# Two layers with sixteen experts each: second layer's results through DRAM, turns grouped anew, residual scale moved

## The chip, the core and the metric

The kernel runs on one core of a Trainium2 chip. Its engines are TensorE (PE; its weight loads are listed apart as PEld), VectorE (DVE), ScalarE (ACT), GpSimd (POOL) and SyncE (SP), which here issues most of the DMAs. Each engine works through its own instructions in order; a DMA queue (SPq, ACTq, POOLq) is fed by the engine that issues the DMAs, in the order of that engine's program. The metric is the device time of one execution in microseconds (us).

## The reference, cut to what matters

Two layers work on 512 latent tokens and 256 context tokens, with 1024 channels. A layer is a mixer (a projection, a recurrent scan, a long convolution and gates), a residual step with a layer norm, then a mixture of experts and a second residual step with a layer norm:

```python
def moe_ffn(h, w_router, router_bias, w_gate, w_up, w_down):
    scores = jax.nn.softmax(h @ w_router, axis=-1)           # 16 experts, 4 groups of 4
    ...                                                       # best group, then its top 2 experts; wts sum to 1
    def expert_block(args):
        xblk, e = args
        return (jax.nn.silu(xblk @ w_gate[e]) * (xblk @ w_up[e])) @ w_down[e]
    ...
    return (y_slots.reshape(n_tok, TOP_K, d) * wts[..., None]).sum(1)

def post_norm(x, s, g, b):                                    # ALPHA = 4 ** 0.25
    return layer_norm(ALPHA * x + s, g, b)                    # layer_norm scales by g and adds b

xl = post_norm(xl, mod_l[2] * mix_l, ln_g[l, 0], ln_b[l, 0])  # after the mixer
...
xl = post_norm(xl, mod_l[5] * yf, ln_g[l, 1], ln_b[l, 1])     # after the experts
```

`mod_l[5]` is the gate of the expert sub-layer, a row of 1024 numbers; the context has a row of its own. Layer 1 computes experts for the 512 latent tokens only, layer 0 for all 768. Every expert has three 1024 x 1024 float32 matrices.

## The kernel before, in words

Each layer runs through projection, scan, merge and experts. In the projection, 1 MB or 0.5 MB pieces of weights come in; ACT casts each to the high part (`hi`, L588), DVE subtracts for the low part (`lo`, L589), and PE multiplies in three passes (L593 to L595 or L848 to L855). ACT takes the sigmoid of the mixer's gates (L1056) and copies rows of modulation (`mrow`, L710) that PE then uses (L722).

**Experts.** The 16 experts are ranked by load. A table `CAPS` gives each rank a number of rows: layer 0 has 96, 256, 192, three of 160, four of 96 and six of 64; layer 1 has 96, 192, 128, five of 96 and eight of 64. A table `TURN` says which ranks are worked side by side. `(2,), (11, 10)` means rank 2 beside a pair: two 64-row experts that share a unit of 128 rows. A unit is up to 128 rows of tokens of one expert or pair. Layer 0 has eight turns, and so has layer 1. A turn gathers the rows of its tokens (POOL, L1874), transposes them, and goes through six chunks per expert: two of the gate matrix, two up (L1950), two down (L1953). In layer 0, 128-row units are worked in three passes from high and low parts. Each chunk needs two buffers of weights, `raw`, of 1 MB each, that SP loads (`weights`); they come from a ring of `RAW` buffers, 5 in layer 0 and 10 in layer 1, and a buffer is loaded again when PE is through with it. A layer loads 192 of them, 201.3 MB.

**Results.** A unit's result rows go back to their tokens in one of two ways. Units of the last `LATE` turns are multiplied by their gates and spread by a one-hot matrix `sel`: for each block of 128 tokens and each half of the channels PE multiplies the high and the low part (L2034, L2035) into `pt`, and DVE adds that to `xs` (L2037), which holds the residual stream. `LATE` is 1 in layer 0 and 99 (all turns) in layer 1. Units of other turns are written to DRAM (`yd`, by the ACT queue, L2074), without the gate. In the last turn of layer 0, `early` has POOL gather two such rows per token (L1772), add them (L1780), multiply by the gate row of the token's kind (L1781) and add to `xs` (L1782). After the second token block the row `grow[1]` is turned into a difference (L1784), from which DVE builds the gates of the last unit's rows (L2050).

**After the experts.** `finish` normalises. In layer 0 POOL then multiplies by the norm's scale and adds its offset (L1818, L1819) for each of four latent blocks, and SP stores that to DRAM (`xd`, L1820), from where layer 1's merge reads it as residual. Layer 1's projection has begun by then on PE, DVE and ACT.

## Time and profile before

| | |
|---|---|
| median of 3 runs | 3294.33 us (3290.19 to 3295.82) |
| profiled execution | 3294.88 us, span 3293.0 us |
| PE busy | 2976.3 us (90%) |
| DVE busy | 1711.4 us (52%) |
| ACT busy | 1143.1 us (35%) |
| POOL busy | 556.0 us (17%) |
| DMA moved | 675.42 MB, mean 205 GB/s |
| expert weights (`raw<-in_w_exp`) | 384 DMAs of 1024 KB |

A busy share over the whole span says little here: the stages have different limits. The page's slices show PE at 90% or more and DMA between 300 and 395 GB/s in the two expert stages (about 1110 to 1765 us and 2670 to 3260 us), and DMA around 50 to 160 GB/s in most of the others. So the tables by stage and by turn below are the ones to read, with the waits and the timeline where a turn is longer than its PE work. A row's `<-` after an idle time names what ended it.

### The profile page before, as it was taken

What the parts mean: (1) busy time and instruction counts of PE and PEld (TensorE: products, weight loads), DVE (VectorE), ACT (ScalarE), POOL (GpSimd) and SP (SyncE); (2) the same over time, 40 slices, a digit from 0 to 9 for tenths busy, and PEclk for the clock granted to TensorE, in tenths of its full rate; (3) what the DMA queues carried; (4) which work ended last, traced back from release to release, by engine and by line L of the source; (5) the groups of instructions that cost most, each with busy time, mean ns of one, the idle gap of its engine ahead of it and who ended that gap; (6) DMA issues with size and microseconds to landing.
All of it is one profiled execution on the core that took longest, in us unless ns stands there. A gap on an engine that the chain in (4) does not pass through costs nothing. (4 is left out here: it accounts for less than half of the span.)

```text
span 3293.0 us, 61763 instructions
## 1 busy us (share of the span) xinstructions
PE 2976.3 (90%) x25406; PEld 2036.7 (62%) x25406; DVE 1711.4 (52%) x3074; ACT 1143.1 (35%) x2309; POOL 556.0 (17%) x436
## 2 busy tenths in 40 slices
PE   8999998988888899999965999989887979999996
PEld 5878865767676555666632767657665745445543
DVE  4466525787758433344407546467885652123343
ACT  3453215655422233344412433265543221111121
POOL 1001213334005100000036001153320210000000
PEclk9999998898999799999996999988898879999998
DMA  5453273111353789988894374431113489888795
GB/s 223 131 157 97 82 260 114 49 47 46 113 195 129 279 331 346 350 328 326 322 392 157 111 218 126 156 119 53 56 50 126 152 327 395 325 303 314 300 360 240
DMA packets 215206, 675.42 MB, mean 205 GB/s; under 512 B 70949, under 2 KB 98886, under 8 KB 163464
## 3 DMA queue, kind: packets, MB, share of 16 engines
q1 hardware_dynamic: 186120, 588.36, 49.4%
q10 hardware_dynamic: 22512, 61.55, 5.3%
q0 software_dynamic: 6288, 21.50, 1.9%
q8 instruction: 203, 3.33, 0.4%
q14 instruction: 83, 0.68, 0.1%
HBM read 615.03 MB, written 56.30 MB: 204 GB/s over the span
## 5 line engine op out<-in xcount | busy, mean ns | idle before, releaser
L1950 PE MATMUL acc<-raw,x 128*32 128x128 f32 (+1 forms) x7168 | 569.5, 333 | 13.5 <-DMA raw<-in_w_exp 12.4
L1950 PEld LDWEIGHTS acc<-raw,x 128*32 128x32 f32 (+1 forms) x7168 | 362.3, 125 | 207.5 <-issue 86.4
L589 DVE TENSOR_TENSOR lo<-raw,hi 128x1024 fp32r<-128x1024 f32 x190 | 230.0, 1230 | 294.9 <-ACT hi L588 282.6
L1953 PE MATMUL acc<-raw,a 128*64 128x512 f32 (+2 forms) x1376 | 300.3, 604 | 2.0 <-DMA raw<-in_w_exp 1.9
L588 ACT CAST hi<-raw 128x1024 fp32r<-128x1024 f32 x190 | 194.7, 1047 | 242.5 <-PE px L852 114.7
L1981 DVE TENSOR_TENSOR act<-acc,act 128x256 f32<-128x256 f32 (+2 forms) x98 | 42.0, 429 | 379.9 <-PE acc L1950 345.1
L848 PE MATMUL pl<-xh,hi 128*128 128x512 f32 x560 | 226.7, 405 | 0.1
L853 PE MATMUL pl<-xh,lo 128*128 128x512 f32 x560 | 223.9, 400 | 0.5 <-DVE lo L589 0.5
L849 PE MATMUL pl<-xl,hi 128*128 128x512 f32 x560 | 222.9, 398 | 0.0
L1953 PEld LDWEIGHTS acc<-raw,a 128*64 128x64 f32 (+2 forms) x1376 | 81.1, 130 | 168.0 <-issue 155.9
L1116 PE MATMUL gp<-gx,raw 128*128 128x512 f32 (+1 forms) x352 | 179.1, 628 | 1.2 <-ACT gs L1118 1.1
L1874 POOL DMA_INDIRECT xg<-hd,idx x31 | 32.0, 1031 | 756.1 <-PE pt L1892 678.5
L848 PEld LDWEIGHTS pl<-xh,hi 128*128 128x128 f32 x560 | 106.1, 189 | 37.6 <-issue 14.3
L1976 ACT ACTIVATE act<-acc 128x256 f32<-128x256 f32 (+2 forms) x98 | 38.0, 388 | 259.5 <-PE acc L1950 216.0
L853 PEld LDWEIGHTS pl<-xh,lo 128*128 128x128 f32 x560 | 106.5, 190 | 17.9 <-issue 9.2
L1999 ACT COPY a<-pt 128x256 f32<-128x256 f32 (+2 forms) x86 | 27.7, 350 | 255.4 <-PE pt L1994 248.5
L849 PEld LDWEIGHTS pl<-xl,hi 128*128 128x128 f32 x560 | 106.0, 189 | 15.8 <-issue 8.1
L311 PE MATMUL pO<-T,K 128*128 128x192 f32 (+1 forms) x320 | 83.4, 372 | 29.9 <-DVE T L330 29.3
L851 PE MATMUL px<-xh,hi 128*128 128x256 f32 x376 | 110.0, 293 | 0.0
L855 PE MATMUL px<-xh,lo 128*128 128x256 f32 x376 | 108.7, 290 | 0.0
L852 PE MATMUL px<-xl,hi 128*128 128x256 f32 x376 | 108.2, 288 | 0.4 <-DVE xl L589 0.3
L2037 DVE TENSOR_TENSOR xs<-pt,xs 128x512 f32<-128x512 f32 x116 | 75.8, 686 | 54.6 <-PE pt L2035 53.8
(611 smaller groups left out, 6200.2 us busy)
## 6 DMA issues: line engine op xcount, KB each, us to landing
raw<-in_w_exp SPq DMA_DIRECT2D x384, 1024.0 KB
mraw<-in_w_mod SPq DMA_DIRECT2D x64, 512.0 KB
raw<-in_w_in SPq DMA_DIRECT2D x36, 512.0 KB
rkk<-rkk SPq DMA_DIRECT2D x24, 768.0 KB
raw<-in_w_in ACTq DMA_DIRECT2D x34, 512.0 KB
mraw<-in_w_mod SPq DMA_DIRECT2D x12, 1024.0 KB
raw<-in_w_in SPq DMA_DIRECT2D x32, 256.0 KB
wb<-in_w_branch SPq DMA_DIRECT2D x32, 256.0 KB
```

What stands on the lines that cost most here:

```text
L311: nc.tensor.matmul(pO[:, jj, 0:192], lO, T[c][kO, j, 1, :], start=True, stop=True)
L588: self.nc.scalar.copy(hi, src)
L589: (engine or self.nc.vector).tensor_tensor(lo, src, f32(hi), ALU.subtract)
L848: mm(pl, hi[:, k], xh[:, k, L], start=f, stop=False)
L849: mm(pl, hi[:, k], xl[:, k, L], start=False, stop=False)
L851: mm(px, hi[:, k], xh[:, k, X], start=f, stop=False)
L852: mm(px, hi[:, k], xl[:, k, X], start=False, stop=False)
L853: mm(pl, lo[:, k], xh[:, k, L], start=False, stop=e)
L855: mm(px, lo[:, k], xh[:, k, X], start=False, stop=e)
L1116: nc.tensor.matmul(p[:, :n], raw[k // 4][:, k % 4], self.gx[:, k, a - T0:a - T0 + n], start=k == 0, stop=k == 7)
L1950: mm(a[w * g:w * g + w, 0:4 * w], x, raw[:, 4 * w * g:4 * w * g + 4 * w], start=k == 0, stop=k == 7)
L1953: mm(a[w * g:w * g + w], x, raw, start=k < G, stop=k >= 8 - G)
```

## The change

- **Turns.** Layer 0 has seven turns: the ranks of 256, 192 and 160 rows each run beside a pair, two with 160 beside 96, and the last is two experts of 96. Layer 1 has seven too: 192, 128 and 96 rows each beside a pair, two of 96 with 96, and a last turn of one pair. The ring of layer 0 has 6 buffers rather than 5.
- **Results of layer 1.** `LATE` is 1 in both layers. `yd` is a list with an array per layer. Layer 1 writes all results but the last unit's to DRAM, and gathers them in its last turn. In layer 0 the last turn has two units where it had one.
- **Gates.** Every unit's result is multiplied by its gate row before it is written or spread, so `early` has two operations per block rather than three, and the difference of the gate rows is formed ahead of the experts. `early` fetches 5 (layer 0) or 4 (layer 1) token blocks ahead rather than 3.
- **Residual scale.** Layer 0's `finish` stores the normalised rows as they are. A new block in layer 1's projection loads each of the four blocks of `xd` by the ACT queue into one buffer `t`, has POOL multiply and add, and stores it back by the ACT queue.
- The rows of `yd` that no unit writes are filled with zero for both layers (POOL's queue).

```diff
-RAW = 5, 10
+RAW = 6, 10
 AHEAD = 2, 2
 CAPS = ([96] + [256] + [192] + [160] * 3 + [96] * 4 + [64] * 6, [96] + [192] + [128] + [96] * 5 + [64] * 8)
-TURN = ([((0,),), ((2,), (11, 10)), ((1,), (13, 12)), ((3,), (6,)), ((4,), (7,)), ((5,), (8,)), ((9,),), ((15, 14),)],
-        [((0,),), ((15, 14),), ((1,), (13, 12)), ((2,), (3,)), ((4,), (5,)), ((6,), (7,)), ((11, 10),), ((9, 8),)])
-LATE = 1, 99
+TURN = ([((0,),), ((1,), (15, 14)), ((2,), (13, 12)), ((3,), (11, 10)), ((4,), (6,)), ((5,), (7,)), ((8,), (9,))],
+        [((0,),), ((1,), (15, 14)), ((2,), (13, 12)), ((3,), (11, 10)), ((4,), (5,)), ((6,), (7,)), ((9, 8),)])
+LATE = 1, 1
...
-SOME, YB, YW = 4, 1, (3, 2)
+SOME, YB, YW = 4, 1, (3, 3)
...
+        self.yd = [self.dt_([128 * rows_of(l)[2] + 1, 1024], f"yd{l}") for l in range(2)]
...
         mod_pools(GMR[l], 2)
+        if l == 1:
+            rs = s_mod.enter_context(tc.tile_pool(name="res", bufs=1))
+            lng, lnb = (rs.tile([128, 1024], F32, name=q, tag=q) for q in ("lng", "lnb"))
+            nc.scalar.dma_start(lng, A["ln_g"][0, 1][None, :].to_broadcast([128, 1024]))
+            nc.scalar.dma_start(lnb, A["ln_b"][0, 1][None, :].to_broadcast([128, 1024]))
+            for tb in range(2, 6):
+                t = rs.tile([128, 1024], F32, name="t", tag="t")
+                nc.scalar.dma_start(t, self.xd[tb])
+                nc.gpsimd.tensor_tensor(t, t, lng, ALU.mult)
+                nc.gpsimd.tensor_tensor(t, t, lnb, ALU.add)
+                nc.scalar.dma_start(self.xd[tb], t)
...
             def fetch(tb):
-                if tb % 3:
-                    y = f32(P["x"].tile([128, 8, 2, 128], F32R, name="x", tag="x256")).rearrange("p a b c -> p (a b c)")
+                if l == 0 and tb % 5:
+                    q = "x" if tb < 3 else "a"
+                    y = f32(P["x"].tile([128, 8, 2, 128], F32R, name=q, tag=q + "256")).rearrange("p a b c -> p (a b c)")
                     y = [y[:, 0:1024], y[:, 1024:2048]]
+                elif l == 1 and tb > 3:
+                    q = "x" if tb == 4 else "a"
+                    y = [P["x"].tile([128, 8, 128], F32, name=q, tag=q + "128", bufs=XB[l]).rearrange("p a b -> p (a b)") for i in range(2)]
                 else:
                     y = [P["x"].tile([128, 1024], F32, name="xg", tag="xg", bufs=XG[l]) for i in range(2)]
                 for i in range(2):
-                    nc.gpsimd.indirect_dma_start(out=y[i], out_offset=None, in_=self.yd, in_offset=bass.IndirectOffsetOnAxis(ap=slot[:, i, tb:tb + 1], axis=0))
+                    nc.gpsimd.indirect_dma_start(out=y[i], out_offset=None, in_=self.yd[l], in_offset=bass.IndirectOffsetOnAxis(ap=slot[:, i, tb:tb + 1], axis=0))
                 ys[tb] = y
 
-            for tb in range(3):
+            n = 5 - l
+            for tb in range(b0, b0 + n):
                 fetch(tb)
             for tb in blocks:
                 y = ys[tb]
                 op = nc.vector.tensor_tensor if tb in EARLY_V else nc.gpsimd.tensor_tensor
                 op(y[0], y[0], y[1], ALU.add)
-                op(y[0], y[0], grow[1 if tb < 2 else 0], ALU.mult)
                 op(self.xs[:, tb], y[0], self.xs[:, tb], ALU.add)
-                if tb == 1:
-                    nc.gpsimd.tensor_tensor(grow[1], grow[1], grow[0], ALU.subtract)
-                if tb + 3 < 6:
-                    fetch(tb + 3)
+                if tb + n < 6:
+                    fetch(tb + n)
...
                     self.normalise(sg, x, x, hs[tb])
                     if tb > 1:
-                        b = sg.tile([128, 1024], F32, name="b", tag="b")
-                        nc.gpsimd.tensor_tensor(b, x, lng, ALU.mult)
-                        nc.gpsimd.tensor_tensor(b, b, lnb, ALU.add)
-                        nc.sync.dma_start(self.xd[tb], b)
+                        nc.sync.dma_start(self.xd[tb], x)
...
         groups = TURN[l]
+        if on:
+            nc.gpsimd.tensor_tensor(grow[1], grow[1], grow[0], ALU.subtract)
...
-        def total(a, w, o, scale):
+        def total(a, w, o):
 
             t = P["a"].tile([128, 512], F32, name="sum", tag="y", bufs=3)[o:o + 64]
-            if w == 64:
-                nc.scalar.activation(t, a[64 - o:128 - o], AF.Copy, scale=scale)
-                return a[o:o + 64], t
             nc.scalar.copy(t, a[64 - o:128 - o])
             tt(t, a[o:o + 64], t, ALU.add)
+            if w == 64:
+                return t
             v = P["a"].tile([128, 512], F32, name="sum", tag="y", bufs=3)[o:o + 32]
-            nc.scalar.activation(v, t[32:64], AF.Copy, scale=scale)
-            return t[0:32], v
+            nc.scalar.copy(v, t[32:64])
+            tt(v, t[0:32], v, ALU.add)
+            return v
...
-                    sel[u] = P["x"].tile([128, 512], F32R, name="sel", tag="sel", bufs=3)
+                    sel[u] = P["x"].tile([128, 512], F32R, name="sel", tag="sel", bufs=1)
...
-                        if dst is None and l == 0:
+                        if l == 0:
                             g[u] = P["a"].tile([128, 512], F32, name="g", tag="act", bufs=ACT_BUFS[l])
                             stt(g[u][0:rows], self.grow[1][0:rows, H], own[:, 2:3], self.grow[0][0:rows, H], ALU.mult, ALU.add)
-                        elif dst is None:
+                        else:
                             g[u] = self.grow[0][:, H]
                 for (u, w, o, *_), a in zip(mine[j], acc):
                     rows, _, own, dst, _ = units[u]
                     R = slice(o, o + w)
                     y, by = out[u][R], own[R, 1:2]
                     if w < 128:
-                        a, t = total(a, w, o, 1.0 if dst is None else by)
-                    if dst is None:
-                        if w < 128:
-                            tt(t, a, t, ALU.add)
-                            a = t
-                        stt(y, a, by, g[u][R], ALU.mult, ALU.mult)
-                    elif w < 128:
-                        stt(y, a, by, t, ALU.mult, ALU.add)
-                    else:
-                        nc.scalar.activation(y, a, AF.Copy, scale=by)
+                        a = total(a, w, o)
+                    stt(y, a, by, g[u][R], ALU.mult, ALU.mult)
```

The line numbers of the changed kernel are shifted (L1950 became L1967, L1953 L1970, L1772 L1791, L1056 L1069).

On POOL, in the last turn of layer 0, this stands before; `xg` and `x` are gathered rows, `g_10143` and `g_10145` the gate rows of the latents and of the context:

```order
L1772 DMA xg<-yd,slot 128x1024 x2
L1772 DMA x<-yd,slot 128x1024 x4
L1780 TENSOR_TENSOR xg<-xg 128x1024
L1772 DMA xg<-yd,slot 128x1024
L1781 TENSOR_TENSOR xg<-xg,g_10145 128x1024
L1772 DMA xg<-yd,slot 128x1024
L1782 TENSOR_TENSOR xs<-xg,xs 128x1024
L1780 TENSOR_TENSOR x<-x 128x1024 x2
L1781 TENSOR_TENSOR x<-x,g_10145 128x1024
L1781 TENSOR_TENSOR x<-x,g_10143 128x1024
L1782 TENSOR_TENSOR xs<-x,xs 128x1024
L1784 TENSOR_TENSOR g_10145<-g_10145,g_10143 128x1024
```

And this now, in the same place:

```order
L1791 DMA xg<-yd_97,slot 128x1024 x2
L1791 DMA x<-yd_97,slot 128x1024 x4
L1791 DMA a<-yd_97,slot 128x1024 x4
L1800 TENSOR_TENSOR xg<-xg 128x1024
L1791 DMA xg<-yd_97,slot 128x1024
L1801 TENSOR_TENSOR xs<-xg,xs 128x1024
L1791 DMA xg<-yd_97,slot 128x1024
L1800 TENSOR_TENSOR x<-x 128x1024 x2
L1801 TENSOR_TENSOR xs<-x,xs 128x1024 x2
```

Ten gathers rather than six are issued ahead, the multiplications by gate rows are gone, and the subtraction no longer stands among them (it is now right behind the stage's first gather of token rows).

On ACT, at the end of layer 1's projection, this stands before; `pl` is PE's product for the latents, `hz` a row of modulation:

```order
L1056 ACTIVATE t_18423<-pl 128x512
L710 COPY mrow<-hz 128x512
L1056 ACTIVATE t_18483<-pl 128x512
L1056 ACTIVATE t_18517<-pl 128x512
L710 COPY mrow<-hz 128x512
L588 CAST hi<-raw 128x1024
L1056 ACTIVATE t_18576<-pl 128x512
```

And this now:

```order
L1052 DMA t<-xd 128x1024
L711 COPY mrow<-hz 128x512
L1055 DMA xd<-t 128x1024
L1069 ACTIVATE t_18666<-pl 128x512
L1052 DMA t<-xd 128x1024
L1069 ACTIVATE t_18700<-pl 128x512
L1055 DMA xd<-t 128x1024
L711 COPY mrow<-hz 128x512
L588 CAST hi<-raw 128x1024
L1052 DMA t<-xd 128x1024
L1055 DMA xd<-t 128x1024
L1069 ACTIVATE t_18759<-pl 128x512
```

The loads and stores of `t` stand among the sigmoids and the copies of `mrow`, the last of them ahead of the last sigmoid.

On PE, where a turn of layer 1 ends and the next begins, this stands before:

```order
L1953 MATMUL acc<-raw,a 64x512 x7
L2034 MATMUL pt<-yh,sel 128x512
L2035 MATMUL pt<-yl,sel 128x512
L2034 MATMUL pt<-yh,sel 128x512
L2035 MATMUL pt<-yl,sel 128x512
L1950 MATMUL acc<-raw,x 128x512
L2034 MATMUL pt<-yh,sel 128x512
L2035 MATMUL pt<-yl,sel 128x512
L2034 MATMUL pt<-yh,sel 128x512
L2035 MATMUL pt<-yl,sel 128x512
L1950 MATMUL acc<-raw,x 128x512 x7
```

And this now, at a turn's end in the same layer:

```order
L1970 MATMUL acc<-raw,a 64x512 x8
L1970 MATMUL acc<-raw,a 128x512 x8
L1970 MATMUL acc<-raw,a 64x512 x16
L1967 MATMUL acc<-raw,x 64x256 x8
L1967 MATMUL acc<-raw,x 32x128 x16
L1967 MATMUL acc<-raw,x 64x256 x8
L1967 MATMUL acc<-raw,x 32x128 x16
```

The products with `sel` that stood between the experts' products are gone.

## Rows read from the trace of the kernel before

**Rows 1.** page, the span

```profile
span 3293.0 us, 61763 instructions
```

**Rows 2.** windows of layer 1's experts: us, busy of each engine, PEclk, DMA share, GB/s

```profile
2669.70:3259.80 590.10, 580.37 (x4720) 301.19 (x4720) 184.88 (x334) 92.38 (x197) 11.77 (x12) 1.00 0.87 334
2711.70:2768.10 56.40, 54.20 (x373) 28.64 (x372) 17.55 (x31) 9.61 (x20) 2.75 (x3) 1.00 1.01 382
...
3069.00:3151.20 82.20, 82.20 (x951) 44.45 (x950) 31.63 (x57) 15.41 (x34) 0.00 (x0) 1.00 0.82 308
...
3204.60:3259.80 55.20, 49.90 (x346) 25.51 (x342) 16.19 (x26) 6.63 (x14) 0.00 (x0) 1.00 0.88 366
3180.00:3200.00 20.00, 18.75 (x109) 7.83 (x105) 5.70 (x9) 3.62 (x7) 0.00 (x0) 1.00 1.01 420
```

**Rows 3.** windows of layer 0's experts: the stage, then five turns

```profile
1110.60:1764.60 654.00, 611.00 (x5373) 384.35 (x5372) 241.34 (x286) 217.96 (x329) 74.75 (x48) 0.98 0.87 332
1154.40:1274.20 119.80, 112.51 (x673) 66.25 (x669) 39.78 (x45) 37.93 (x55) 3.73 (x3) 0.99 0.87 333
1274.20:1389.80 115.60, 115.07 (x657) 80.15 (x657) 39.55 (x42) 38.77 (x54) 2.78 (x3) 1.00 0.91 350
1389.80:1474.60 84.80, 84.79 (x923) 55.92 (x921) 41.81 (x47) 38.91 (x57) 2.72 (x3) 1.00 0.88 329
...
1640.60:1676.80 36.20, 35.96 (x466) 20.26 (x462) 5.79 (x10) 7.42 (x16) 0.00 (x0) 1.00 0.96 374
1676.80:1764.60 87.80, 54.77 (x344) 26.66 (x340) 22.51 (x26) 6.72 (x14) 56.86 (x31) 0.88 0.82 325
```

**Rows 4.** lines, layer 1's experts: the one-hot products

```profile
L2034 PE MATMUL pt<-yh,sel 96*128 96x512 f32 (+2 forms) x104 | 47.6, 468 | 8.4 <-ACT yh L588 7.8 <-DVE xs L2037 0.7
```

**Rows 5.** PE's timeline, two token blocks: start, us, instructions

```profile
2712.71 0.50 PE L2034 MATMUL pt<-yh,sel 96*128 96x512 f32 x1
...
2713.83 2.38 PE L1950 MATMUL acc<-raw,x 128*64 128x256 f32 x20
```

**Rows 6.** timeline of layer 0's last turn, POOL and DVE

```profile
1689.17 0.94 POOL L1772 DMA_INDIRECT xg<-yd,slot  x1 [0.30 <-issue]
...
1700.87 2.37 POOL L1780 TENSOR_TENSOR xg<-xg 128x1024 f32<-128x1024 f32 x1 [5.79 <-DMA xg<-yd,slot]
...
1728.77 1.41 DVE L2050 SCALAR_TENSOR_TENSOR g<-g,own,g 128x512 f32<-128x512 f32 x2 [31.70 <-POOL g L1784]
```

**Rows 7.** waits of PE, 1680 to 1780: total us, times, longest

```profile
PE pt L1994 <- DVE act L1981: 15.0, 4, 12.3
PE acc L1950 <- DMA raw<-in_w_exp: 12.0, 8, 1.9
```

**Rows 8.** timeline where layer 0 ends, POOL and DVE

```profile
1785.18 2.36 POOL L1818 TENSOR_TENSOR b<-xs,lng 128x1024 f32<-128x1024 f32 x1 [25.43 <-ACT xs L1380]
...
1787.93 2.38 DVE L1428 TENSOR_SCALAR q<-q 64x512 f32<-64x512 f32 x1
...
1803.65 4.67 DVE L589 TENSOR_TENSOR xl<-xt,xh 128x512 fp32r<-128x512 f32 x2
...
1815.40 0.41 DVE L1428 TENSOR_SCALAR q<-q 64x512 f32<-64x512 f32 x1
1815.73 0.68 DVE L589 TENSOR_TENSOR xl<-xt,xh 128x512 fp32r<-128x512 f32 x1
```

**Rows 9.** timeline of layer 1's gates, PE, ACT and POOL

```profile
2137.88 1.02 PE L722 MATMUL pq<-mrow,con 128*2 128x512 f32 x2 [0.70 <-ACT mrow L710]
...
2147.29 0.60 ACT L1056 ACTIVATE t<-pl 128x512 f32<-128x512 f32 x1 [8.52 <-issue]
...
2147.27 0.30 POOL L224 MEMSET PB<- 64x256 f32 x1 [39.24 <-PE pl L853]
```

**Rows 10.** timeline of SP's queue at the end

```profile
3282.53 0.33 SPq L1830 DMA_DIRECT2D out<-b  x1
```

**Rows 11.** window behind that store

```profile
3285.00:3286.00 1.00, 0.00 (x0) 0.00 (x0) 0.00 (x0) 0.00 (x0) 0.00 (x0) 0.50 0.02 8
```

More of the change, by code (lines that the diff above doesn't have):

```diff
@@ L659, in setup @@
         self.xd = self.dt_([6, 128, 1024], "xd")
-        self.yd = self.dt_([128 * rows_of(0)[2] + 1, 1024], "yd")
+        self.yd = [self.dt_([128 * rows_of(l)[2] + 1, 1024], f"yd{l}") for l in range(2)]
     def layer(self, l):
@@ L688, in zero_unused @@
         nc.gpsimd.memset(zero, 0.0)
-        base, nsb, first = rows_of(0)
-        used = {(b + 32 * i) // 32 for b, c in zip(base, CAPS[0]) for i in range(c // 32)}
-        for q in range(4 * first):
-            if q not in used and (q % 4 == 0 or q - 1 in used):
-                n = next((i for i in range(1, 4 - q % 4) if q + i in used), 4 - q % 4)
-                for h in range(2):
-                    nc.gpsimd.dma_start(self.yd[32 * q:32 * q + 32 * n, 512 * h:512 * h + 512], zero[0:32 * n])
-        for h in range(2):
-            nc.gpsimd.dma_start(self.yd[128 * first:128 * first + 1, 512 * h:512 * h + 512], zero[0:1])
+        for l in range(2):
+            base, nsb, first = rows_of(l)
+            used = {(b + 32 * i) // 32 for b, c in zip(base, CAPS[l]) for i in range(c // 32)}
+            for q in range(4 * first):
+                if q not in used and (q % 4 == 0 or q - 1 in used):
+                    n = next((i for i in range(1, 4 - q % 4) if q + i in used), 4 - q % 4)
+                    for h in range(2):
+                        nc.gpsimd.dma_start(self.yd[l][32 * q:32 * q + 32 * n, 512 * h:512 * h + 512], zero[0:32 * n])
+            for h in range(2):
+                nc.gpsimd.dma_start(self.yd[l][128 * first:128 * first + 1, 512 * h:512 * h + 512], zero[0:1])
     def mod(self, l, n, wr, sm, acc_, small, kk, dma, tag="mraw"):
@@ L1599, in unit @@
             return (rows, *((idx[0:rows, q:q + 1], own[0:rows, :, q]) if q else (idx0[0:rows], own0[0:rows])),
-                    None if q >= first else self.yd[128 * q:128 * q + rows], shared)
+                    None if q >= first else self.yd[l][128 * q:128 * q + rows], shared)
         units = {ranks: [unit(min(128, (len(ranks) * caps[ranks[0]]) - 128 * i), base[ranks[0]] // 128 + i, len(ranks) > 1) for i in range(-(-caps[ranks[0]] // 128))]
```

7 lines of the change are left out of this document (4 added, 3 removed).

## The prediction, made before the changed kernel ran

> **What bounds the kernel now.** I read the page first, then tables by stage, then the waits and timelines of the places that the change touches. The profiled execution took 3294.9 us, of which its span is 3293.0 [rows 1] and 1.9 lies around it; the median of the runs is 3294.3. The sum is made against 3294.9, and 0.6 goes off at the end. A run of this kernel can tell about 0.2%, 6.6 us, from no change.
>
> The two expert stages are 654.0 and 590.1 us. In layer 1 PE is busy 580.4 of 590.1 us at full clock, and DMA at a share of 0.87 and 334 GB/s [rows 2]: PE is the bound, but the weight stream is close behind, and in the turns of light experts both are full (382 GB/s at a share of 1.01). In layer 0 PE is busy 611.0 of 654.0 [rows 3]. Most of what is missing lies in the last turn, 87.8 us long with PE busy 54.8.
>
> **Layer 1: block adds go.** Today each 128-row result is spread over the tokens by one-hot products: 104 at L2034 [rows 4] and as many at L2035. Two blocks take 2712.71 to 2713.83, 1.12 us [rows 5], so a block costs PE 0.56 us, one after the other with the expert products. The change keeps the last unit's 8, so 96 x 0.56 = 53.8 us leave PE. The casts, DVE additions and one-hot rows that go with them lie beside PE and count nothing. In their place come 12 half-row writes of results and, in the last turn, 8 gathers (4.2 MB), with 8 POOL operations of 2.4 us [rows 6]: 19 us beside a turn of some 50, hidden.
>
> Then what is late next? PE would need 590 - 54 = 536 us. The stage moves 334 GB/s x 590.1 us = 197.1 MB; with 5.5 MB of writes and 4.2 MB of gathers it is 206.8 MB. At the 420 GB/s of one stretch that is 492 us, at the 382 of a whole turn 541 [rows 2]. So for most of the stage the stream keeps up, but the last turn, now the only one made of light experts, needs 25.2 + 4.2 + 0.5 = 29.9 MB in 46 to 50 us of PE: 73 us at 410 GB/s, less at most 26 us for ten buffers loaded ahead. The earlier heavy turns give that lead (the 127 us turns have 25.2 to 37.7 MB). What PE then waits in it, by this bookkeeping turn by turn (the light turns before it eat part of the lead, the 96 + 96 turns give it back): 5 us at 410, 14 at 400, 35 at 380. Today's last turn already lacks 5.3 of PE. I take a wait between the first two, 12, which is 7 more than today, and 2 us for DVE held by POOL: 54 - 7 - 2 = **45 us gained**; ends 24 (380 GB/s: 54 - 35 + 5) and 57 (no wait, today's 5.3 partly gone).
>
> **Layer 0: turns grouped anew.** Eight turns become seven; three (119.8, 115.6, 84.8), the single expert (36.2) and the light pair (87.8) are rebuilt [rows 3]; the other three, 209.8 us, keep their shapes. New ones:
> - 256 rows with a pair: the row of the same make is 115.6, with PE full: 117 (ends 115 and 122).
> - 192 with a pair: today 119.8 with PE busy 112.5; I put what is missing down to the five buffers, and there are six now: 108 (112 is that busy time; 104 lies between the 94 that 160 rows with a pair need, below, and the 115 of 256 rows).
> - 160 with a pair: PE needs the 84.8 of 160 + 96 rows, less 36.2 for the 96, and a pair, which is 49.9 in layer 1's last turn less its 8 blocks x 0.56, 45.4 [rows 2]: 94. The stream for three experts is 37.75 MB, times 217.1/201.3 for what else moves (332 GB/s x 654 us = 217.1 MB; the weights are 201.3) = 40.7 MB, or 102 us at 400 GB/s, less a few of lead: 98 (94 to 104).
> - 96 with 96: 2 x 36.2 + 12 blocks x 0.56 = 79.1; stream 25.2 + 6.3 of gathers = 31.5 MB, 79 us at 400: 82 (79 to 88).
>
> Sum 209.8 + 117 + 108 + 98 + 82 = 614.8 against 654.0: 39 less. What goes is the stall in today's last turn: the gather chain on POOL scales and subtracts the gates (L1781, L1784), and DVE at L2050 waits 31.7 us for that [rows 6], behind which PE stands 12.3 us for its activations; another 12.0 us PE waits for weights [rows 7]. In the changed kernel the subtraction is issued ahead of the experts, behind the first gather of rows. I give back 3 us for a longer tail (two units' adds after the last product rather than one) and 5 for the added DVE work (a gate row per unit and half, DVE being busy 241 of 654 us) and POOL against DVE: **31 us gained**; ends 10 (all upper, 636 + 8) and 49 (all lower, nothing given back).
>
> **The boundary.** After layer 0, POOL multiplies and adds L1818 and L1819 eight times from 1785.18 on. Beside it DVE runs slowly: L1428 takes 2.38 us against 0.41 alone, two L589 4.67 against 2 x 0.68 [rows 8]. Seven such instructions lose about 11 us there, by these ratios, and PE waits for some of them. I take **7 gained** (0 to 11). The Trainium skill, "SBUF — State Buffer", section "Who interferes with whom", says that a VectorE instruction with two SBUF inputs and a GpSimd one reading SBUF shut each other out. The 4.67 agrees; so does what follows, that the same eight POOL operations cost something again where they are put.
>
> **Layer 1's projection: the scaling goes there.** POOL stands idle 39.24 us up to 2147.27 [rows 9], so its work (4 x 2 x 2.4 = 19 us) is free. The queue is not. Loads and stores are issued by ACT, in its order, one buffer `t`: each load waits for the store before, each store for POOL. The trace of before has no such chain; the nearest rows bound it. Lower: the last store of the output is issued at 3282.53 [rows 10], and by 3285.0 the DMA moves 8 GB/s [rows 11], so 0.5 MB takes 2.5 us, and with its return I take 4. Upper: a gather issued at 1689.17 releases its user only at 1700.87 [rows 6], 11.7 us. With 4: three first loads 5.5 + 4 x 4.8 + 3 x (4 + 4) = 48.7 us from 2108.0, so the last store is issued at 2156.7. ACT's sigmoid of 2147.29 [rows 9] stands behind it, 9.4 us late. Also behind waiting ACT: the copy of `mrow`, which PE's L722 waits for (0.70 today [rows 9]), the weight casts, and through the last gates the scan's start. With 1.5 us for DVE held by POOL: **11 lost**. Ends: 0 (loads landed ahead, ACT waits absorbed by its idle 8.52) and 7 x 11.7 + 19.2 = 101 us of chain less the 39 of idle = 62.
>
> Twelve more zero fills, other buffers of the one-hot rows and the two smaller constants fewer cost nothing that I can find: POOL is busy 17% of the span, and the fills are issued where it idles.
>
> **Sum.** -31 - 7 + 11 - 45 = -72: 3294.9 - 72 = 3222.9, and on the median's scale 3222.
>
> **Rivals.**
> *The stream binds from above.* If DMA in a whole stage can't pass about 358 GB/s, layer 0 is 217.1/0.358 = 606 us, still under PE's 614.8, but layer 1 is 206.8/0.358 = 578: 12 gained rather than 45; total -31 - 7 + 11 - 12 = -39, 3256. At the 350 GB/s of a turn with PE full [rows 3] layer 0 is 620 and layer 1 591: -26 - 7 + 11 + 1, 3273. For it: no whole stage passes 334. Against it: whole turns at 382 with a share of 1.01 and 20 us at 420 [rows 2]. The Trainium skill, "DMA: Bandwidth & Descriptors", section "Where 436 GB/s comes from", says that between HBM and SBUF the HBM side binds, at about 358 GB/s per core, and by that this rival holds; the page's own single-core figure of 425 for large transfers, and the 420 of this trace, with one core at work, disagree. Chance 0.08.
> *Layer 0's regrouping yields little.* Turns with three experts starve on their buffers, as the 119.8 us one did today (7.3 short of PE): with 122, 120, 104 and 88 the stage is 643.8, and with 5 given back 649: 5 gained, not 31, and in all 3248. For it: the weights come two buffers at a time, and six buffers hold three such steps; against: the 115.6 turn with three experts and PE full [rows 3]. Chance 0.12.
> *ACT's queue stands still.* Each 0.5 MB takes 11.7 us: +62 instead of +11, 3273. For: the gather row; against: gathers are row by row, these are plain. Chance 0.06.
> *Slower.* The stream can't rise over the mean of before, since its pace is set by how it is issued, buffer by buffer, and not by what PE asks: then layer 0 takes 217.1/0.332 = 654, no gain, and layer 1 206.8/0.334 = 619, 29 longer; with -7 + 11 the total is 3328. It decides from a pace below 342 GB/s: the two stages carry 423.9 MB, and may take 1244 - 4 = 1240 us until nothing is gained. For: both stages show 332 and 334. Against: 308 GB/s at a share of 0.82 with PE full all 82.2 us [rows 2], a stream that waits for PE. Chance 0.04.
>
> **Chances and range.** The forecast has 0.70, with its own range from 3200 to 3250 (a little inside both expert stages near their best ends and near their worst). The range to hold 8 in 10 runs from 3190 (layer 0 at -49, layer 1 at -57, the rest as summed: 3192) to 3264 (layer 0 at -10, layer 1 at -24, the rest as summed), which takes in the first two rivals. All cases but the last are faster by more than 6.6 us: faster 0.95, same 0.01, slower 0.04.
>
> **What would show it.** Right: layer 1's expert stage 540 to 548 us, with PE full until the last turn and then short by some 10, and DMA over 360 GB/s; layer 0's 615 to 630 with no long DVE wait in the last turn; DVE's L589 at 0.68 each at the start of layer 1; ACT idle on the DMA of `t` between 2108 and 2157 of the old time and PE's L722 late by about 10. Wrong: PE waits for weights through both stages (stream), PE waits in the three-expert turns of layer 0 (second rival), or a gap of tens of us before the scan (third).

## The result, and the profile after

The changed kernel takes 3258.5 us (median of 4 runs, 3250.1 to 3266.0), against 3295.1 before: a ratio of 0.989 (95% interval 0.985 to 0.992). In five later runs it was 3253.3 and 0.987 (0.985 to 0.989). So it is some 37 to 42 us faster: inside the range, but a little over half of the 72 that were forecast. The first profiled execution took 3266.0 us, the slowest of its four; a second one, from the later runs, spans 3245.2. Both stand in the table, because they help to tell a cost from chance. The times are read from PE's instructions.

| us | before | after, first | after, second |
|---|---|---|---|
| start of the span to layer 0's first expert product | 1110.6 | 1111.2 | 1100.8 |
| layer 0's experts, to the last product | 653.9 | 644.2 | 641.3 |
| from there to the last block add | 8.9 | 21.4 | 21.4 |
| to the first full product of layer 1's projection | 50.0 | 38.7 | 37.8 |
| projection, to its 198th hi x hi product | 251.2 | 251.6 | 250.2 |
| projection, to its last such product | 71.6 | 86.8 | 85.5 |
| to the scan's main loop (L417) | 69.8 | 72.8 | 73.7 |
| scan | 252.4 | 255.6 | 251.7 |
| merge, to the router (L1337, now L1350) | 144.9 | 147.7 | 145.7 |
| to layer 1's first expert product | 56.1 | 56.5 | 57.1 |
| layer 1's experts, to the last product | 590.1 | 543.8 | 545.0 |
| to the end of the span | 33.2 | 33.7 | 34.9 |

Layer 1's experts gave the time that was forecast. Layer 0's gave nothing: 9.7 us up to the last product, and 12.5 taken back behind it. The residual scale cost more where it was put than it freed where it was.

Layer 1's expert stage of the changed kernel, by windows (columns as in [rows 2]): the stage, the turn of 128 rows with a pair, the one of 96 with a pair, the last.

```profile
2686.50:3230.00 543.50, 519.37 (x4529) 264.34 (x4528) 98.44 (x168) 79.06 (x173) 37.94 (x28) 1.00 0.95 380
...
2837.90:2928.90 91.00, 89.59 (x450) 43.11 (x450) 10.32 (x16) 9.69 (x20) 1.83 (x2) 1.00 1.01 413
2928.90:3019.70 90.80, 83.56 (x801) 42.64 (x797) 16.53 (x27) 13.95 (x31) 0.95 (x1) 1.00 1.00 409
...
3165.90:3230.00 64.10, 48.67 (x340) 24.30 (x336) 15.54 (x24) 6.58 (x14) 26.60 (x16) 1.00 0.95 387
```

PE's busy time fell from 580.4 to 519.4 [rows 2], the stream rose from 334 to 380 GB/s, with two turns over 400. What is short of PE's work now is 24 us, 15.4 of it in the last turn.

Layer 0's turns in the changed kernel, in the same columns: 256 rows with a pair, 192 with a pair, 160 with a pair, and the last (96 and 96) up to its last product.

```profile
1157.30:1272.40 115.10, 115.10 (x660) 80.45 (x657) 50.49 (x58) 36.73 (x51) 2.74 (x3) 1.00 0.88 341
1272.40:1383.70 111.30, 108.06 (x671) 64.56 (x669) 47.08 (x56) 33.31 (x51) 3.67 (x3) 1.00 0.95 363
1383.70:1499.30 115.60, 105.98 (x795) 63.39 (x795) 49.56 (x59) 36.24 (x55) 2.73 (x3) 0.96 0.92 349
...
1667.30:1755.40 88.10, 77.72 (x929) 41.92 (x925) 39.16 (x50) 13.12 (x30) 40.93 (x24) 0.96 0.79 320
```

The third row is the surprise: 115.6 us where 98 were forecast, with DMA at a share of 0.92 and only 349 GB/s.

Behind the last product, DVE (start, duration, instruction, idle time before and what ended it):

```profile
1762.54 1.29 DVE L2054 TENSOR_TENSOR xs<-pt,xs 128x512 f32<-128x512 f32 x2 [0.23 <-PE pt L2052]
1763.75 2.46 DVE L1825 BATCH_NORM_STATS2 bs<-xs 128x6 f32<-128x512 f32 x4
1766.12 0.73 DVE L2076 SCALAR_TENSOR_TENSOR y<-sum,own,g 64x512 f32<-64x512 f32 x1
...
1768.96 0.74 DVE L2076 SCALAR_TENSOR_TENSOR y<-sum,own,g 32x512 f32<-32x512 f32 x1
```

and PE:

```profile
1762.37 0.50 PE L2051 MATMUL pt<-hi 96*128 96x512 f32 x1
1762.70 0.39 PE L2052 MATMUL pt<-lo,hi 96*128 96x512 f32 x1
1770.46 0.80 PE L2051 MATMUL pt<-hi 96*128 96x512 f32 x1 [7.37 <-ACT hi L588]
```

The two last units finish together, but the second one's rows (L2076) are built only behind the first one's six block adds and their statistics. PE stands 7.4 us, and then runs the second unit's adds alone.

At the start of layer 1, DVE's L1428 (now L1441) runs without POOL beside it, at 0.36 rather than the 2.38 of [rows 8]:

```profile
1789.06 0.36 DVE L1441 TENSOR_SCALAR q<-q 64x512 f32<-64x512 f32 x1
...
1798.44 1.29 DVE L589 TENSOR_TENSOR xl<-xt,xh 128x512 fp32r<-128x512 f32 x2 [0.84 <-ACT xh L588]
```

From the last block add to the first full product of the projection, before and now (columns as in [rows 2], DVE's busy time is the third of the engines'):

```profile
1773.70:1823.60 49.90, 21.31 (x89) 14.28 (x90) 43.89 (x81) 20.98 (x33) 22.27 (x8) 0.59 0.34 115
1776.80:1815.50 38.70, 21.76 (x89) 15.07 (x89) 32.64 (x81) 20.89 (x34) 0.00 (x0) 0.59 0.44 149
```

In the projection, ACT's timeline, where `mrow` stands behind a store of `t`, and PE's waits from 2067 to 2154 (total, times, longest):

```profile
2143.09 0.33 ACTq L1055 DMA_DIRECT2D xd<-t  x1
2143.46 0.59 ACT L711 COPY mrow<-hz 128x512 f32<-128x512 f32 x1 [8.80 <-POOL t L1054]
...
2154.32 0.33 ACTq L1055 DMA_DIRECT2D xd<-t  x1
2154.91 0.60 ACT L1069 ACTIVATE t<-pl 128x512 f32<-128x512 f32 x1 [9.92 <-PE pl L854]
```

```profile
PE pq L723 <- ACT mrow L711: 7.4, 1, 7.4
PE hz L709 <- DMA mraw<-in_w_mod: 3.5, 1, 3.5
```

```profile
2130.00:2140.00 10.00, 6.71 (x34) 3.51 (x32) 0.00 (x0) 0.60 (x1) 1.69 (x1) 1.00 0.91 312
2140.00:2150.00 10.00, 5.90 (x9) 1.69 (x10) 1.81 (x2) 1.53 (x2) 3.56 (x3) 0.50 0.66 224
```

The last row is the window in which PE waits: its granted clock is 0.50 there, the lower of the two levels, behind 10 us in which PE was busy 6.71. The projection's last part as a whole, before and now, with a clock of 1.00 and of 0.90:

```profile
2074.70:2146.40 71.70, 67.77 (x317) 45.45 (x316) 23.88 (x36) 18.37 (x26) 7.59 (x7) 1.00 0.55 180
2067.20:2154.00 86.80, 74.14 (x317) 46.93 (x316) 26.05 (x36) 18.26 (x26) 27.05 (x15) 0.90 0.59 203
```

### The profile page after: what moved, and what is told of

It is laid out like the page before. It is cut to its first block, busy times and chain, and to the rows that moved or that the text cites. A ratio compares the mean times of both kernels' runs of the same rounds, so it can differ in the third digit from the quotient of the medians.

```text
span 3264.0 us, 61452 instructions
## 1 busy us (share of the span) xinstructions
PE 2947.1 (90%) x25238; PEld 2019.3 (62%) x25238; DVE 1689.8 (52%) x3009; ACT 1116.9 (34%) x2275; POOL 574.1 (18%) x458
## 5 line engine op out<-in xcount | busy, mean ns | idle before, releaser
L1967 PE MATMUL acc<-raw,x 128*64 128x256 f32 (+1 forms) x7168 | 569.6, 334 | 14.1 <-DMA raw<-in_w_exp 13.5
L1967 PEld LDWEIGHTS acc<-raw,x 128*64 128x64 f32 (+1 forms) x7168 | 358.1, 125 | 214.5 <-issue 88.4
L589 DVE TENSOR_TENSOR lo<-raw,hi 128x1024 fp32r<-128x1024 f32 x190 | 230.1, 1234 | 287.4 <-ACT hi L588 280.1
L1970 PE MATMUL acc<-raw,a 128*64 128x512 f32 (+2 forms) x1376 | 293.6, 602 | 8.0 <-DMA raw<-in_w_exp 8.0
L1998 DVE TENSOR_TENSOR act<-acc,act 128x256 f32<-128x256 f32 (+1 forms) x98 | 42.0, 429 | 442.8 <-PE acc L1967 400.6
L1970 PEld LDWEIGHTS acc<-raw,a 128*64 128x64 f32 (+2 forms) x1376 | 79.1, 130 | 180.4 <-issue 159.8
L1993 ACT ACTIVATE act<-acc 128x256 f32<-128x256 f32 (+1 forms) x98 | 38.1, 388 | 240.6 <-PE acc L1967 201.7
L2022 DVE TENSOR_TENSOR sum<-acc,sum 64x512 f32<-64x512 f32 x82 | 56.3, 687 | 118.7 <-ACT sum L2021 118.0
```

The costliest lines, as they stand in the source:

```text
L589: (engine or self.nc.vector).tensor_tensor(lo, src, f32(hi), ALU.subtract)
L1967: mm(a[w * g:w * g + w, 0:4 * w], x, raw[:, 4 * w * g:4 * w * g + 4 * w], start=k == 0, stop=k == 7)
L1970: mm(a[w * g:w * g + w], x, raw, start=k < G, stop=k >= 8 - G)
```

## The experiments

Numbers of stages are read as in the table above. Ratios are to the kernel before.

**Half of layer 0's weights.** What do its turns take when the stream can't bind?

```diff
+        if l == 0 and half:
+            return self.raw0
-        raw = P["wr"].tile([128, 4, 512], F32, name="raw", tag="raw")
+        raw = self.raw0 = P["wr"].tile([128, 4, 512], F32, name="raw", tag="raw")
```

> The changed kernel, but in layer 0's expert stage the second 1 MB buffer of every chunk is not loaded: the first one is multiplied twice, so half of that layer's weights don't move and the numbers differ. PE's, ACT's and DVE's instructions stay. In the changed kernel's trace the stage went, turn by turn, 46.1, 115.1, 111.3, 115.6 (160 rows with a pair), 85.7, 82.3 and 88.1 us to the last product, 644. Theory A (the weight stream binds the three-expert turns and the last one; the prediction's 400 GB/s was too much for this layer, where the turn of 115.6 us moved 349 GB/s at a share of 0.92): 160 rows with a pair falls to 94 to 100, the last turn to 80 to 83, 256 and 192 rows with a pair to 113 and 105; 44 to 46, 85 and 82 stay; together 600 to 612. Theory B (the casts on ACT and DVE, or PE's own work, bind them): each turn stays within 3 us, stage 636 to 644. The tail behind the last product (21 us) stays under both.

Measured (one run): the stage takes 602.7 us, turn by turn 43.6, 115.0, 102.9, 93.0, 83.6, 82.3, 82.3; the tail is 21.4 as in the changed kernel. Here the whole stage, 160 rows with a pair, and the last turn:

```profile
1113.00:1715.60 602.60, 597.23 (x5377) 383.72 (x5377) 317.28 (x376) 212.96 (x317) 58.65 (x41) 0.99 0.55 191
1374.50:1467.40 92.90, 92.90 (x796) 59.90 (x794) 49.97 (x58) 38.20 (x54) 3.29 (x3) 1.00 0.68 229
1633.30:1715.60 82.30, 76.93 (x929) 42.59 (x925) 51.28 (x50) 13.11 (x30) 39.90 (x24) 0.96 0.44 170
```

Theory A holds: 41.5 us of the changed stage (38.6 of the second trace's) are the loading of weights, 22.6 of them in the one turn of 160 rows with a pair. PE's own work there was forecast well (94 against 92.9); the stream's pace was not. Half the loads also let six buffers reach twice as far, so this run does not tell a slow stream from a short ring.

**Layer 0's old turns**, all else as changed.

```diff
-TURN = ([((0,),), ((1,), (15, 14)), ((2,), (13, 12)), ((3,), (11, 10)), ((4,), (6,)), ((5,), (7,)), ((8,), (9,))],
+TURN = ([((0,),), ((2,), (11, 10)), ((1,), (13, 12)), ((3,), (6,)), ((4,), (7,)), ((5,), (8,)), ((9,),), ((15, 14),)],
```

> The changed kernel with layer 0's TURN table as it was before (eight turns, a light pair alone in the last), all else as changed (six buffers, gates per unit, early subtraction). Theory A (the regrouping brings nothing: it trades the light pair's waits for waits of the 160-row turn with a pair, and pays a longer tail): layer 0 from the first expert product to the last block add takes 645 to 655 us rather than 665.6, since the DVE wait in the last turn is gone here too; whole kernel 8 to 18 us below the changed one, 3240 to 3250. Theory B (the prediction's: the regrouping gains some 30 us, and something else ate it): 680 to 695 us, whole kernel 15 to 30 above the changed one, 3273 to 3288.

Measured: 3237.4 us (3230.3 to 3238.2), 0.982 (0.978 to 0.985). Layer 0 takes 635.6 to the last product and 9.5 behind it, 645.1 in all, against 665.6 and 662.7 in the changed kernel's two traces. The whole is 16 to 21 us faster than the changed kernel, a little more than theory A's 8 to 18. The last turn is

```profile
1669.60:1745.20 75.60, 52.08 (x344) 24.89 (x340) 19.37 (x28) 6.58 (x14) 40.08 (x24) 0.98 0.89 364
```

against 87.8 in [rows 3]. So theory A: the regrouping itself costs 18 to 21 us. What gained in layer 0 are the other edits. The last turn is 12.2 shorter: PE waits 2.4 us for `act` there rather than the 15.0 of [rows 7], though 17.4 for weights rather than 12.0. And 192 rows with a pair take 112.0 rather than 119.8, with the sixth buffer.

**Loads and stores of `t` by POOL's queue.**

```diff
-                nc.scalar.dma_start(t, self.xd[tb])
+                nc.gpsimd.dma_start(t, self.xd[tb])
-                nc.scalar.dma_start(self.xd[tb], t)
+                nc.gpsimd.dma_start(self.xd[tb], t)
```

> The changed kernel with the loads and stores of t in layer 1's projection issued by GpSimd's queue rather than ACT's. In the changed kernel's trace the stretch from the first product of the last weight block's neighbours to the first gate product of the merge lost 15 us there (69.5 against 54.0) and 18 by the start of the scan. Theory A (ACT waits for t's transfers, and PE for what stands behind it on ACT): PE's wait for mrow of 7.4 us goes, the stretch takes 54 to 58, whole kernel 10 to 18 us below the changed one, 3240 to 3249. Theory B (what costs is POOL's operations holding DVE, and the transfers beside the weight loads, whatever queue issues them): the stretch stays over 64, whole kernel within 6 of the changed one.

Measured: 3267.5 us (3251.8 to 3275.4), 0.990 (0.988 to 0.993), no gain. PE's wait for `mrow` did fall, from 7.4 to 0.7 us, and the projection's last part from 86.8 to 81.5. But the way to the scan grew from 72.8 to 88.1. POOL's timeline shows why:

```profile
2146.02 0.58 POOL L1055 DMA_DIRECT2D xd<-t  x1 [0.30 <-POOL t L1054]
2149.50 0.55 POOL L1052 DMA_DIRECT2D t<-xd  x1 [2.89 <-DMA xd<-t]
...
2159.70 0.34 POOL L224 MEMSET PB<- 64x256 f32 x1
```

The fills for the scan stand behind POOL's own waits: they start 15.3 us after the projection's last product, against 0.5 in the changed kernel. Neither theory had that wait; the time only moved.

**One-hot products again in layer 1**, with the new turns.

```diff
-LATE = 1, 1
+LATE = 1, 99
-SOME, YB, YW = 4, 1, (3, 3)
+SOME, YB, YW = 4, 1, (3, 2)
-                    sel[u] = P["x"].tile([128, 512], F32R, name="sel", tag="sel", bufs=1)
+                    sel[u] = P["x"].tile([128, 512], F32R, name="sel", tag="sel", bufs=3)
```

> The changed kernel with layer 1's results again spread by one-hot products in every turn (no writes to yd and no gathers in layer 1, three buffers of one-hot rows, two of results), turns of layer 1 as changed. Theory A (the block adds were on PE's path, 0.56 us each): layer 1's expert stage, 543.8 us in the changed kernel and 590.1 before, takes 585 to 592. Theory B (what gained was the new order of turns, which lets the stream run ahead): 545 to 560. With shares of both: 565 to 580.

Measured (one run): 3309.0 us. The stage, its turn of 192 rows with a pair (110.00 us in the changed kernel), and its last turn (64.10 there):

```profile
2676.90:3274.80 597.90, 589.19 (x4720) 302.07 (x4720) 183.76 (x333) 92.06 (x197) 11.27 (x12) 1.00 0.87 329
2719.20:2847.20 128.00, 128.00 (x662) 63.14 (x660) 35.42 (x62) 16.45 (x33) 1.83 (x2) 1.00 0.84 311
...
3220.70:3274.80 54.10, 51.03 (x349) 26.47 (x348) 19.11 (x31) 6.61 (x14) 0.00 (x0) 1.00 0.77 308
```

The stage is 54.1 us above the changed kernel's 543.8. Theory A, and a little past its upper end. The prediction's 96 x 0.56 was 53.8, but the two are not the same thing. The turns up to the last, with 90 block adds in them, are 64.4 us longer here, 0.72 us per block; the last turn is 10.0 shorter, since PE doesn't wait for weights in it. So 54.1 is the price of the block adds less what came late once they were gone. The new turns alone, with block adds, are 7.8 slower than the old ones.

**Layer 1's old turns**, results through DRAM.

```diff
-        [((0,),), ((1,), (15, 14)), ((2,), (13, 12)), ((3,), (11, 10)), ((4,), (5,)), ((6,), (7,)), ((9, 8),)])
+        [((0,),), ((15, 14),), ((1,), (13, 12)), ((2,), (3,)), ((4,), (5,)), ((6,), (7,)), ((11, 10),), ((9, 8),)])
```

> The changed kernel with layer 1's TURN table as it was before (a light pair first, two light pairs one after the other at the end), results still through DRAM with gathers. With one-hot products the changed table took 597.9 us and the old one 590.1, so where PE binds, the new table costs 8. Theory A (once the block adds are gone the stream binds in the light turns, and the new table, which puts the pairs beside heavy experts, is what lets the loads run ahead): the stage from the first to the last product takes 555 to 580 us against 543.8, with PE waiting for weights in the last two turns. Theory B (the order doesn't matter, or costs here too): 530 to 545.

Measured (one run): the stage is 554.2, 10.4 above the new turns; just under the span given by theory A, with its signs: the two light pairs at the end take 54.3 and 70.8 us for 47 and 50 of PE, at DMA shares of 1.02 and 0.95:

```profile
3101.40:3155.70 54.30, 47.16 (x342) 23.69 (x339) 9.45 (x16) 7.70 (x16) 0.00 (x0) 1.00 1.02 422
3155.70:3226.50 70.80, 50.49 (x336) 24.60 (x336) 12.79 (x21) 5.38 (x12) 26.13 (x16) 1.00 0.95 392
```

So the new turns need the other edit: they lose 7.8 where PE binds and gain 10.4 once the stream does. Results through DRAM gain 35.9 with the old turns too.

**Scale in the merge**, no block in the projection.

```diff
+        if l == 1:
+            ...
+            for tb in tbs:
+                nc.gpsimd.tensor_tensor(self.xs[:, tb], self.xs[:, tb], l0, ALU.mult)
+                nc.gpsimd.tensor_tensor(self.xs[:, tb], self.xs[:, tb], b0_, ALU.add)
```

> The changed kernel without the block in layer 1's projection: the merge of layer 1, which loads xd into xs anyway, has POOL multiply and add there, in place, with two more constant rows loaded by ACT's queue. No further load, store or wait on ACT in the projection. Theory A (the chain of transfers through the one buffer t is what costs 18 us, by whichever queue): the projection's last part (198th product to the last) takes 70 to 74 us rather than 86.8, the way to the scan 68 to 73, the merge stays within 4; whole kernel 12 to 20 us below the changed one: 3238 to 3247 on the scale of the first runs. Theory B (POOL beside DVE costs wherever it stands): the merge takes 8 to 12 more, and the whole gains 3 to 8.

Measured: 3259.4 us (3245.1 to 3265.8), 0.987 (0.985 to 0.990), no gain. The projection's last part is 72.0, what it was before the change, so the block, POOL's work and the transfers together, is worth 14 to 15 there. But the merge takes 164.7 rather than 147.7:

```profile
PE po L594 <- DVE ol L589: 15.2, 1, 15.2
```

DVE's low casts for PE stand behind its additions to `xs`, which wait for POOL. The way to the scan is 72.5, no shorter than with the block.

**Both: old turns in layer 0, scale in the merge.**

> Layer 0's old turns (as in the second run) and the scale in the merge (as in this call's second), all else as changed. If the two are independent, the gains add: 21 and 12 to 20 below the changed kernel, 3217 to 3226; if the gain of one is taken by a clock that falls elsewhere or by a wait that both share, 3228 to 3237.

Measured: 3243.3 us (3229.3 to 3260.2), 0.984 (0.979 to 0.988). Layer 0 is 636.3 + 9.5, the merge 170.1: one gain and one loss, as each alone, so the sum of 3217 to 3226 fell with the sixth run, and the total lies above the other range too.

**Five buffers in layer 0.**

```diff
-RAW = 6, 10
+RAW = 5, 10
```

> The changed kernel with 5 buffers of weights in layer 0 rather than 6, its new turns kept. Theory A (the stage is bound by the bytes that a turn moves at 350 to 360 GB/s; the ring only carries lead over): the 160-row turn with a pair stays within 4 us of 115.6, and the stage to the last product within 8 of 644, some 2 to 8 longer. Theory B (the ring starves the three-expert turns, since weights come two buffers at a time): each of the three turns grows by 5 to 10 and the stage is 660 to 675.

Measured (one run): the stage is 648.0, 3.8 longer than in the first trace. 192 and 160 rows with a pair:

```profile
1273.70:1394.30 120.60, 112.53 (x671) 65.61 (x669) 48.79 (x58) 35.45 (x53) 3.66 (x3) 0.99 0.87 336
1394.30:1506.80 112.50, 102.93 (x795) 61.10 (x795) 49.50 (x59) 36.32 (x55) 2.72 (x3) 0.98 0.94 357
```

The sixth buffer is worth 9 us in the turn of 192 rows and nothing in that of 160, which is no longer with five. Theory A for the stage, B for one turn.

Inside the changed kernel's turn of 160 rows the stream is uneven (four stretches of 10 us):

```profile
1413.00:1423.00 10.00, 8.07 (x83) 4.79 (x80) 2.69 (x5) 3.62 (x7) 0.00 (x0) 1.00 1.00 367
1423.00:1433.00 10.00, 10.00 (x81) 7.16 (x74) 4.80 (x6) 2.54 (x4) 0.00 (x0) 0.83 0.69 256
...
1453.00:1463.00 10.00, 9.16 (x64) 5.28 (x63) 6.47 (x10) 5.73 (x10) 0.95 (x1) 1.00 1.01 410
1463.00:1473.00 10.00, 10.00 (x49) 4.57 (x47) 6.13 (x8) 2.21 (x4) 0.00 (x0) 1.00 0.75 269
```

In these two stretches with PE full DMA falls to a share of 0.69 and 0.75; in the two where DMA is at 1.00 PE is not full. So 349 GB/s is the mean of a stream that pauses at times, and the stream reaches 410 in this layer too. Pauses while PE works are what a short ring would give, as the second rival had it; that the same turn was no longer with five buffers speaks against it.

**Eight half pieces through three buffers**, with old turns in layer 0; first with stores by ACT, then by POOL's queue.

```diff
-                t = rs.tile([128, 1024], F32, name="t", tag="t")
-                nc.scalar.dma_start(t, self.xd[tb])
+                for H in HH:
+                    t = rs.tile([128, 512], F32, name="t", tag="t", bufs=3)
+                    nc.scalar.dma_start(t, self.xd[tb, :, H])
...
+                    nc.scalar.dma_start(self.xd[tb, :, H], t)
```

> Layer 0's old turns, and the block in layer 1's projection worked in eight pieces of 512 columns through three buffers t of half the size, loads and stores still issued by ACT. Theory A (the serial chain of load, POOL, store through one buffer sets the delay): loads overlap POOL, so the chain is about 8 x 2.4 us of POOL and a few us at each end, 26 to 36 us inside the 47 that are there; the projection's last part takes 73 to 79 rather than 86 to 90, whole kernel 8 to 16 below the second run (old turns alone, 3237): 3221 to 3229. Theory B (ACT's waits for POOL before each store, now eight rather than four, cost as much): 84 to 92, no gain.

> As the kernel before in this call, but the eight stores of t are issued by GpSimd's own queue, so that ACT waits only where a buffer is not free for the next load. Theory A: 72 to 77 for the projection's last part, and up to 3 us more by the scan's start since POOL issues eight more DMAs ahead of its fills; whole kernel 10 to 18 below old turns alone, 3219 to 3227. Theory B (the queue of GpSimd is slow, as in the third run, and its fills come late): the way from the last product to the scan grows from 72 to over 78, no gain.

Measured: 3236.4 us, 0.982 (0.980 to 0.985), and 3237.4, 0.982 (0.979 to 0.984): old turns alone, no more. In the first, POOL is through long before its next work (1.29 us from 2116.64, then idle):

```profile
2116.64 1.29 POOL L1055 TENSOR_TENSOR t<-t,lnb 128x512 f32<-128x512 f32 x1
2131.22 0.30 POOL L224 MEMSET PB<- 64x256 f32 x1 [13.29 <-DMA raw<-in_w_in]
```

POOL's chain ends early, and still the projection's last part is 85.7 us, against 89.8 in the second run; in the other kernel it is 82.4, without ACT in PE's way but with PE waiting for its own weights:

```profile
PE hz L709 <- DMA mraw<-in_w_mod: 7.3, 3, 4.0
```

That was 1.4 before the change. Theory A of both runs falls: the serial chain was not the whole cost. The first fits its theory B, with 5.6 us of waits for `mrow`; the second doesn't, since its way to the scan is 72.4.

**The changed kernel again.**

> The changed kernel unaltered, on the chip of this call, as the yardstick for the other two: 0.985 to 0.992 of before, and by stage what its first trace showed within 4 us: layer 0's experts 644 and 21 behind them, the projection's last part 87, layer 1's experts 544. If the scan and the merge take 252 and 145 here (they took 256 and 148 in its first trace, 252 and 145 before), their 6 us were chance and no cost of the change.

Measured: 3253.3 us (3247.3 to 3258.4), 0.987 (0.985 to 0.989), and the stages of the third column above. The scan's 251.7 and the merge's 145.7 make the 6 us there in the first trace chance: over all traces that leave these two stages as they are, their sum goes from 396.6 to 406.3.

**Old turns, scale first of all in the merge**, two blocks on DVE and two on POOL.

```diff
+            for tb in range(2, 6):
+                op = nc.vector.tensor_tensor if tb < 4 else nc.gpsimd.tensor_tensor
+                op(self.xs[:, tb], self.xs[:, tb], l0, ALU.mult)
+                op(self.xs[:, tb], self.xs[:, tb], b0_, ALU.add)
```

> Layer 0's old turns, no block in layer 1's projection, and the scale in layer 1's merge as in the sixth run, but first of all there: xs and the two constants are loaded ahead of the merge's other rows, two blocks are scaled by DVE and two by POOL, ahead of POOL's preparation of the rows. In the sixth run the merge lost 17 us (164.7 against 147.7), since PE waited 15.2 for DVE's low casts, behind DVE additions that waited for POOL's blocks. Theory A (that order was the cost): the merge takes 145 to 154, the projection's last part 71 to 73, whole kernel 3220 to 3230, below both kernels and the second run. Theory B (the loads of xs come too late at that place, whatever the order): the merge takes 158 to 168, whole kernel 3232 to 3242.

Measured: 3234.5 us (3226.5 to 3241.2), 0.981 (0.979 to 0.984). The projection's last part is 72.3, the merge 159.7: theory B by its numbers, though what comes late is the constants rather than `xs`. DVE waits for them, and its casts run slowly beside POOL:

```profile
DVE xs L1265 <- DMA lng<-in_ln_g: 8.7, 1, 8.7
```

```profile
2579.10 5.48 DVE L589 TENSOR_TENSOR ol<-wo,oh 128x1024 fp32r<-128x1024 f32 x2
```

(two such take 2.35 at 2591.49 of the same trace). This kernel beats both. So do three of the other four with layer 0's old turns; the interval of the fourth (0.979 to 0.988) meets the changed kernel's. Among these five the runs show no difference.

## Why the prediction was half right

**Layer 1's experts, -45: the time right, its parts in some measure by luck, measured -46.3 and -45.1.** The wait for weights in the last turn came as taken: of its 15.4 us without PE work 12.7 are such waits, against 12. But a block add cost 0.72 us rather than 0.56, so the turns up to the last gained 64.4 and not some 50; the last turn then lost 10.0; and the new order of turns took 7.8 that stand nowhere in the sum. 64.4 - 10.0 - 7.8 is 46.6. Where the extra 0.16 per block comes from no run shows. That the order of turns is worth 10.4 once the adds are gone was in the forecast only as lead.

**Layer 0's experts, -31: wrong, measured +2.8 and -0.1 with the tail.** Three terms failed. First, "160 with a pair ... 102 us at 400 GB/s, less a few of lead: 98" took 115.6 (112.6 to 115.6 over six traces): PE needs 92.9, but the turn's 40.3 MB came at 349 GB/s. The 400 was between 382 and 420 of layer 1 [rows 2]; layer 0's own busiest rows, 350 and 374 [rows 3], were the nearer ones. At 350 the same 40.3 MB are 115 us. Second, the last turn took 88.1 to the last product, not 82; with half the weights it took 82.3. Third, "3 us for a longer tail" was 12.5: the two units end together, and on DVE, which works in order, the second's rows stand behind the first's adds. These are 17.6, 6.1 and 9.5 us; the other turns came out 5.7 longer, about the 5 that the sum had given back for DVE. The stall that was to go did go; the second run shows 12 us for it with the old turns. It was paid for twice by the new ones. PE's wait in a three-expert turn, which the prediction had named as a sign of being wrong, came: 9.9 us for casts of weights with 160 rows. The second rival had the sum nearly (5 gained) and named these turns, though not their times (120 for 192 rows, 104 for 160). Its reason, starving on the ring, is shown for 192 rows (9 us from five to six buffers) and not for 160.

**The boundary, -7: right in kind, measured -11.3 and -12.2.** DVE's busy time there fell by 11.3 us, from 43.9 to 32.6, and the stretch by as much. So it is the whole slowing of DVE beside POOL that goes, the 11 of the prediction's ratios, where the sum had taken 7. The Trainium skill, "SBUF — State Buffer", section "Who interferes with whom", says that a DVE instruction with two SBUF inputs contends with a POOL instruction that reads SBUF. L589 agrees: two took 4.67 us beside POOL and 1.29 now.

**The projection, +11: the place was right, the size was not.** Its last part took 15.2 us more (13.9 in the second trace, 13.5 to 18.2 over all seven that have this block as it stands). The way to the scan took 3.0 more as well, but the kernels without the block have 71.8 to 72.5 there too, so that is not the block's. PE's wait for `mrow` came, 7.4 where 0.7 was and some 10 were written. The last store, at 2154.3, was 5 us later than written, since this part begins 7.5 us sooner than before; the sigmoid behind it is 15.1 late, not 9.4. Not in the sum: PE then ran at a lower granted clock (busy 74.1 us rather than 67.8 in the same work, at a mean of 0.90 rather than 1.00), and its own weights came 2.1 us later. These three, 6.7, 6.3 and 2.1, make 15.1 of the 15.2. The third, ninth and tenth runs, with other queues and further buffers, leave 10 to 14 us of it; the sixth shows that it goes when the block goes. That run takes out the transfers and POOL's work together, and no run parts the two. Since boundary and projection are one edit, moving the scale gained 11 to 12 and cost 14 to 18: it should have been forecast as one exchange. In the merge it cost 12 to 24.

**What of the -72.** First trace: -46 (layer 1), +3 (layer 0), -11 (boundary), +15 (projection), +3 on the way to the scan, +6 by chance in scan and merge, +2 elsewhere: about -29 by the spans. The medians, -37 and -42, lean less on one trace. 3258 lies outside the 3200 to 3250 that had the 0.70, close to the first rival's 3256. That is chance: the rivals on the stream's whole pace fell. Layer 1's stage moved 380 GB/s. The Trainium skill, "DMA: Bandwidth & Descriptors", section "Where 436 GB/s comes from", has the HBM side bind at about 358 GB/s; with one core at work, whole turns here moved 409 and 413. The slower rival had asked for less than 342 in both stages; layer 0 did stay at 335. Two slips in the working changed nothing: layer 0's best end with nothing given back is 52, not 49, and the writes of results are 24, not 12, with about the bytes that were taken.

Open: why the stream in layer 0, with six buffers, does not pass 379 GB/s over any turn of the runs, where layer 1 with ten passes 410. The pauses of DMA while PE is full point at the ring, but no run had a seventh buffer, so that it is the ring was not shown. How much of the lower clock in the projection follows from the wait for `mrow` and how much from the late weights is not settled either: in the tenth run the one was gone and the clock's mean 0.94.

## What to carry to other kernels

Price a stream by the rows of its own stage and ring, not by the best stretch elsewhere: 350 rather than 400 GB/s took back some 24 of 39 us of gain. When work is put beside other work, write down each turn's bytes and PE's time next to each other; a regrouping that evens out PE can undo the evenness of the stream. A pass over data that is moved to an idle engine brings its loads and stores with it: count them against the weights of the place where they land, and set the move's cost beside what the old place cost. A difference between two whole stages holds the new waits too: compare turn by turn before taking it for the price of one instruction.

## Not expected

POOL beside DVE shows in the last turn of layer 0 too: building four `sel` rows took DVE 4.93 us beside POOL's adds and two took 0.48 without:

```profile
1730.60 4.93 DVE L2040 TENSOR_SCALAR hi<-io,own 96x128 fp32r<-96x128 f32 x4
...
1743.00 0.48 DVE L2040 TENSOR_SCALAR hi<-io,own 96x128 fp32r<-96x128 f32 x2
```

And the code ahead of layer 0's experts, nearly the same in all these kernels, took 1100.8 to 1117.8 us from one traced execution to the next. Runs of one kernel spread by up to 1%, so gains of 10 us were read from stages, not from totals.
